# Attention in a decoder trunk: the second head's scaling behind the closing additions, and two weight casts ahead of copies at its beginning

## The chip, the cores and the metric

The kernel runs on one core of a Trainium2 chip. The metric is the device time of one execution in microseconds (us), and of several executions the median. One execution was also taken with the profiler; all rows below come from that one.

## The reference, cut to what matters

For one layer, with 2048 rows of 1024 columns, 16 query heads and 2 key/value heads of 64, and a window of 128 keys:

```python
shift, scale, gate = jnp.split(jax.nn.silu(c) @ w_ada[l] + b_ada[l], 3, axis=-1)
u = x * (1.0 + scale[:, None, :]) + shift[:, None, :]
q, k, v, a_gate, p_in, p_gate, m_a, m_p = jnp.split(u @ w_in[l], offsets, axis=-1)
a = sliding_window_sink_attention(q, k, v, sinks[l], bias, mask) * jax.nn.silu(a_gate)
a = a @ w_attn_proj[l]
p = jnp.einsum('bsgc,gcd->bsgd', multiscale_causal_pool(p_in), w_pool_mix[l]).reshape(B, S, POOL_WIDTH)
p = (p * pool_scale[l]) * jax.nn.silu(p_gate)
p = p @ w_pool_proj[l]
y = (jax.nn.sigmoid(m_a) * a + jax.nn.sigmoid(m_p) * p) @ w_out[l] * (1.0 + gate[:, None, :])
x = layer_norm(DEEPNORM_ALPHA * x + y, ln_gain[l], ln_bias[l])
```

The attention of a block of 128 queries is a softmax over 256 keys plus one sink term, with a bias by distance. The division by the softmax's sum is the scaling that this change moves.

## The kernel before, in words

All matrix products are made with 32-bit numbers that are split into a high and a low part (`low`, line 131, is the subtraction that makes the low part), and each product is three matmuls: high by high, high by low, low by high. A pair of weight rows (a "quad") is multiplied with the halves of `u` by Strassen-like sums: seven block products named B11, T1, T2, B21, T3, B22 and T4 instead of eight. Each block product is 12 matmuls of 128x512 that accumulate in a PSUM bank. After T2 comes a closing addition, b = c + p5, after T3 another, p5 = c + p5, both on VectorE. The T3 product accumulates on the same bank c that T2's addition reads, so its first matmul waits for that addition.

The sequence is computed in two halves. Each half has a stage of gate products (`ring`, with `gate_quad`, whose `consume` applies Silu to a finished product at line 585) and then an `attention` stage. In the trace the first attention stage runs from about 250 to 606 us and the second from about 826 to 1184 us.

`attention` has 67 steps of the loop over n. There are 64 units of work (8 head pairs by 8 blocks of 128 queries), and each is pipelined over four steps. In step n TensorE does, in this order: the scores of unit n (4 matmuls into bank lg), the transposes of unit n-2 (4 into bank pt, the first of the first head, the second of the second head, and so on in turn), a share of the block products of the next weights ("fill", 15 or 18 matmuls), and the value products of unit n-2 (4 into bank pv). VectorE does, in program order: the reciprocal of unit n-1's sums, the additions that gather the output of unit n-3, two passes that add the bias to unit n's scores, the low part `ptl` of unit n-2's transposed weights, and then `tensor_scalar` on `E[:, 1]`, which scales the second head of unit n-1 by that reciprocal. The first head is scaled by ScalarE. In the trace both write the tile L; the transposes of this unit in the next step read it. Behind this scaling, still in step n, the fill issues what belongs to the finished block products: closing additions, low parts of weights, and in `take_q` (for query weights) the high part of two heads on ScalarE and the low part on VectorE, 64x512 each, tile qs.

The wrapper class `Ordered` (names act, dve, pool, pe, sp) keeps an instruction where the program has it on its engine; what is issued through `nc.scalar` and the like may be moved by the scheduler.

At the beginning of `attention` (before the loop) stand the exponential on a one-element tile that loads its function table, `seed(0)` (copies the bank of B11 into the bank in which T2 accumulates), the copy `p5` of T1's bank, and `split` for the first three block products, T2, B21 and T3: a cast of the weight block to its high part on ScalarE and the low part on GpSimd.

Of the kernel before, what the change touches and what calls it, by code (L numbers as in the profile page):

```python
# [14 lines left out]
AF = mybir.ActivationFunctionType  # L15
ALU = mybir.AluOpType
# [43 lines left out]
def kernel(  # L60
# [22 lines left out]
    nc = tc.nc  # L83
    pe, act, dve, pool, sp = (Ordered(tc, e) for e in (nc.tensor, nc.scalar, nc.vector, nc.gpsimd, nc.sync))
# [45 lines left out]
    def low(engine, dst, src, hi):  # L130
        engine.tensor_tensor(dst, src, as32(hi), ALU.subtract)  # L131
# [320 lines left out]
    def defer(ticks, f):  # L452
        due.append((now[0] + ticks, len(due), f))
# [127 lines left out]
    def gate_quad(s, name, base, m, kind):  # L581
        def consume(ph, mi, t, src):
            g = ph.c("sig")
            if kind:
                nc.scalar.activation(g, src, AF.Silu)
                if kind == "scaled":
                    nc.vector.tensor_scalar(g, g, psc[:, m + mi : m + mi + 1], None, ALU.mult)
            else:
                nc.scalar.copy(g, src)
            defer(2, lambda: sp.dma_start(gates_d[name][s, m + mi, t], g))  # L590

        return Quad((win[base + m], win[base + m + 1]), consume)
# [179 lines left out]
    def attention(ph, s, fills, post, opened):  # L772
# [10 lines left out]
        def bias_tile(j):  # L783
            bt = tp.tile([P, 2, 2 * P], F32, tag="bt", bufs=2, name="bt")
            e_src = e_rep[:, 2 * j : 2 * j + 2, :]
            sp.dma_start(bt, bass.AP(e_src.tensor, e_src.offset + P - 1, [[HEADS * ET - 1, P], [ET, 2], [1, 2 * P]]))
            return bt
# [92 lines left out]
        splits = {}  # L880
# [5 lines left out]
        for x, (kind, m, _) in enumerate(fills):  # L886
            if kind == "mix" and POOL_W[m // 2] >= 8:
                on_dve |= {(x, "T3"), (x, "T4"), (x + 1, "T2"), (x + 1, "T3")}

        def split(i):  # L890
            x, name = seq[i]
            q = quads[x]
            if name == "B11" and x > 1:
                q.sum1(pool)
            w = ph.split()
            hi, lo = made[i] = w[:, 0:CH], w[:, CH:]
            act.copy(hi, q.block(name))
            low(dve if name == "T1" or (x, name) in on_dve else pool, lo, q.block(name), hi)
            if name == "T1":
                q.mid(pool)  # L900
            elif name == "B21":
                q.late(pool)
# [18 lines left out]
        def seed(x):  # L921
            st[x][2] = bank()
            act.copy(st[x][2], st[x][0])

        def ended(i):
            x, name = seq[i]
            if x >= K or name == "B11":
                return
            a, b, c, p5 = st[x]
            if name == "T1":  # L930
                p5 = st[x][3] = tp.tile([P, CH], F32, tag="p5", bufs=2, name="p5")
                act.copy(p5, b)
            elif name == "T2":
                dve.tensor_tensor(b, c, p5, ALU.add)
            elif name == "T3":
                dve.tensor_tensor(p5, c, p5, ALU.add)
            elif name == "B21":
                take(x, 0, 0, a)
            elif name == "B22":
                take(x, 0, 1, b)  # L940
            else:
                take(x, 1, 0, c)
                take(x, 1, 1, p5, True)
# [40 lines left out]
        U = 2 * NB  # L984
        load_kv(s)
        bts = {0: bias_tile(0)}
        act.activation(warm, mhalf, AF.Exp)
        seed(0)
        p5 = st[0][3] = tp.tile([P, CH], F32, tag="p5", bufs=2, name="p5")
        act.copy(p5, st[0][1])  # L990
        for i in range(-3, 0):
            for j in splits.get(i, ()):
                split(j)
        fill = filling()
        lgs, exps, Ls, pvs, outs, ags = {}, {}, {}, {}, {}, {}
        total, done = 4 * len(seq), 0
# [1 line left out]
        for n in range(N + 3):  # L998
            now_n[0] = n
            j, t, b = n // U, n // NB % 2, n % NB  # L1000
            if n < N:
                lgs[n] = score_mms(j, n % U, b, qs[j, t])
            pt = None
            if n - 2 in Ls:
                L, k0 = Ls.pop(n - 2)
                pt = turn_mms(L, k0)
            if n - 1 in exps:
                sm = exps[n - 1][2]
                dve.reciprocal(sm, sm)
            if n - 3 in pvs:  # L1010
                pv = pvs.pop(n - 3)
                jj, tt, bb = (n - 3) // U, (n - 3) // NB % 2, (n - 3) % NB
                if bb == 0:
                    outs[jj, tt] = tp.tile([P, CH], F32, tag="o", bufs=2, name="o")
                if bb == 1:
                    ags[jj, tt] = ld("ag", gates_d["ag"][s, jj, tt], 1)
                o2 = tp.tile([HD, 2, P], F32, tag="o2", bufs=1, name="o2")
                act.copy(o2, pv[HD:])
                for h in range(2):
                    dve.tensor_tensor(  # L1020
                        outs[jj, tt][h * HD : (h + 1) * HD, bb * P : (bb + 1) * P], pv[0:HD, h, :], o2[:, h, :], ALU.add
                    )
            if n - 1 in exps:
                E, e0, sm = exps[n - 1]
                act.activation(E[:, 0, e0:256], E[:, 0, e0:256], AF.Copy, scale=sm[:, 0:1])
            if pt is not None:
                h0 = k0 // P
                pth = tp.tile([P, 2, 2, P], F32R, tag="pth", bufs=1, name="pth")
                ptl = tp.tile([P, 2, 2, P], F32R, tag="ptl", bufs=1, name="ptl")
                act.copy(pth[:, h0:], pt[:, h0:])  # L1030
            if n < N:
                lg, c0 = lgs.pop(n)
                L = tp.tile([P, 2, 260], F32, tag="L", bufs=3, name="L")
                nm = tp.tile([P, 2], F32, tag="nm", bufs=4, name="nm")
                sm = tp.tile([P, 2], F32, tag="sm", bufs=4, name="sm")
                act.copy(L[:, :, 256], nsink[:, 2 * j : 2 * j + 2])
                for h in range(2):
                    dve.tensor_tensor_reduce(
                        L[:, h, c0:256],
                        lg[:, h, c0:],  # L1040
                        bts[j][:, h, c0:],
                        1.0,
                        nsink[:, 2 * j + h : 2 * j + h + 1],
                        ALU.add,
                        ALU.min,
                        nm[:, h : h + 1],
                    )
                    act.activation(
                        L[:, h, c0:257],
                        L[:, h, c0:257],  # L1050
                        AF.Exp,
                        bias=nm[:, h : h + 1],
                        scale=-1.0,
                        accum_out=sm[:, h : h + 1],
                    )
                exps[n] = (L, c0, sm)
            if pt is not None:
                low(dve, ptl[:, h0:], pt[:, h0:], pth[:, h0:])
            if n - 1 in exps:
                E, e0, sm = exps.pop(n - 1)  # L1060
                dve.tensor_scalar(E[:, 1, e0:256], E[:, 1, e0:256], sm[:, 1:2], None, ALU.mult)
                Ls[n - 1] = (E, e0)
            while done < -(-total * (n + 1) // (N + 3)):
                next(fill)
                done += 1
            if pt is not None:
                pvs[n - 2] = value_mms((n - 2) % U, k0, pth, ptl)
            run_coming()
            if n % U == 2 and j + 1 < KT:
                bts[j + 1] = bias_tile(j + 1)  # L1070
            for x in [x for x in outs if n == x[0] * U + x[1] * NB + NB + 2]:
                o = outs.pop(x)
                pool.tensor_tensor(o, o, ags.pop(x), ALU.mult)
                later(n + 1, lambda x=x, o=o: keep_raw(ain_d[s], *x, o))
            if n == 28:
                if s:
                    sp.dma_start(as32(kk[:, :, 0:P]), k_d[0, :, :, 2 * CH :])
                sp.dma_start(as32(kk[:, :, P : P + CH]), k_d[s, :, :, P : P + CH])
            if n == 30:
                if s:  # L1080
                    sp.dma_start(as32(vv[:, 0]), v_d[0, :, 2 * NB])
                sp.dma_start(as32(vv[:, 1 : 1 + NB]), v_d[s, :, 1 : 1 + NB])
            if n == 31:
                sp.dma_start(as32(kk[:, :, P + CH :]), k_d[s, :, :, P + CH :])
            if n == 33:
                sp.dma_start(as32(vv[:, 1 + NB :]), v_d[s, :, 1 + NB :])
# [465 lines left out]
    with Pools("mix", spare=4, p=2, c=8) as ph:  # L1552
# [10 lines left out]
        for n, (raw, i) in enumerate((raw, i) for raw in (ain_d[1], pin_d[1], wo_d) for i in range(4)):  # L1563
            for offset, f in sums_to(ph, raw, i, load_raw(raw, i)):
                at = int(2 + 8 * n + offset)
                i, gi = every[at // 14]
# [78 lines left out]
```

## Time and profile before

| what | value |
|---|---|
| median of 3 runs | 1693.99 us (1690.03 to 1697.75) |
| the profiled execution | 1691.31 us |
| its span, first to last instruction | 1689.5 us |
| TensorE busy | 1647.0 us, 97% |
| VectorE busy | 1204.8 us, 71% |
| ScalarE busy | 1021.7 us, 60% |
| GpSimd busy | 995.3 us, 59% |
| granted TensorE clock, mean | 0.996 |

The span and the busy times are from the profiled execution, whose own time lies 1.8 us above its span. PE is TensorE, PEld its weight loads, DVE VectorE, ACT ScalarE, POOL GpSimd. In a row of the timeline stand the start, the length, the engine, the line, the operation, the written tile, an arrow, the tiles read, and how many instructions the row joins; in brackets how long the engine had been idle before it and what it waited for. Most rows show line 56, a helper's line, so that the tiles' names tell the operation.

### The profile page before, as it was taken

What the parts mean: (1) busy time and instruction counts of PE and PEld (TensorE: products, weight loads), DVE (VectorE), ACT (ScalarE), POOL (GpSimd) and SP (SyncE); (2) the same over time, 40 slices, a digit from 0 to 9 for tenths busy, and PEclk for the clock granted to TensorE, in tenths of its full rate; (3) what the DMA queues carried; (4) which work ended last, traced back from release to release, by engine and by line L of the source; (5) the groups of instructions that cost most, each with busy time, mean ns of one, the idle gap of its engine ahead of it and who ended that gap; (6) DMA issues with size and microseconds to landing.
All of it is one profiled execution on the core that took longest, in us unless ns stands there. A gap on an engine that the chain in (4) does not pass through costs nothing.

```text
span 1689.5 us, 24673 instructions
## 1 busy us (share of the span) xinstructions
PE 1647.0 (97%) x8058; PEld 1384.2 (82%) x8058; DVE 1204.8 (71%) x2140; ACT 1021.7 (60%) x2142; POOL 995.3 (59%) x734
## 2 busy tenths in 40 slices
PE   7999999999999999999999999999999999999997
PEld 6788888888888888888788888888878877888886
DVE  6955655776857657357467677675679997989877
ACT  4644547778777756334578777776546445645452
POOL 3343347586866838762376858587567667533442
PEclk9999999999999999999999999999999999999999
DMA  9688843333423468875542334223979797878443
GB/s 360 203 260 310 212 162 107 113 126 112 150 100 107 131 233 312 271 242 181 198 138 87 126 130 136 102 93 131 325 250 392 257 372 255 323 274 280 150 150 113
DMA packets 188850, 336.80 MB, mean 199 GB/s; under 512 B 18336, under 2 KB 44080, under 8 KB 188720
## 3 DMA queue, kind: packets, MB, share of 16 engines
q1 hardware_dynamic: 185600, 330.96, 57.2%
q10 hardware_dynamic: 3088, 4.23, 1.1%
q8 instruction: 64, 1.05, 0.2%
q14 instruction: 66, 0.54, 0.1%
q0 software_dynamic: 32, 0.02, 0.0%
HBM read 227.96 MB, written 110.33 MB: 200 GB/s over the span
## 4 chain that ended last, share of the span: by engine, by line
PE 67%; DVE 12%; DMA 7%; issue 5%; ACT 5%; POOL 4%; SPq 1%; POOLq 0%; DVEq 0%; ACTq 0%
PE mm L56 44%; PE lg L56 16%; PE pv L56 4%; PE pt L56 3%; DVE w_set L131 3%; DVE set_T L56 2%; DVE set_B L56 1%; ACT L L56 1%; DMA g<-ma_d 1%; DMA g<-mp_d 1%; POOL spare L56 1%; DVE w_set L56 1%; ACT w_set L56 1%; DVE wide L627 1%; DMA W<-in_win_dram 1%
## 5 line engine op out<-in xcount | busy, mean ns | idle before, releaser
L56 PE MATMUL mm<-set_B,w_set 128*128 128x512 f32 x2664 | 655.3, 393 | 2.2 <-DVE w_set L131 1.6
L56 PEld LDWEIGHTS mm<-set_B,w_set 128*128 128x128 f32 x2664 | 497.1, 189 | 106.2 <-DVE w_set L131 3.0
L56 PE MATMUL mm<-set_T,w_set 128*128 128x512 f32 x1824 | 454.3, 395 | 6.3 <-DVE mm L56 3.9
L56 PE MATMUL lg<-set_T,w_set 128*128 128x512 f32 x1704 | 412.0, 391 | 10.1 <-DVE w_set L131 5.7
L56 PEld LDWEIGHTS mm<-set_T,w_set 128*128 128x128 f32 x1824 | 335.9, 188 | 76.5 <-DVE mm L56 6.5
L56 PEld LDWEIGHTS lg<-set_T,w_set 128*128 128x128 f32 x1704 | 319.5, 188 | 81.1 <-DVE w_set L131 6.9
L131 DVE TENSOR_TENSOR w_set<-W,w_set 128x1024 fp32r<-128x1024 f32 x138 | 203.2, 1474 | 137.6 <-ACT w_set L305 124.1
L305 ACT CAST w_set<-W 128x1024 fp32r<-128x1024 f32 x138 | 144.8, 1050 | 215.4 <-PE mm L56 134.1
L56 POOL TENSOR_TENSOR w_set<-W,w_set 128x512 fp32r<-128x512 f32 x120 | 157.3, 1319 | 116.5 <-ACT w_set L56 114.6
L268 POOL TENSOR_TENSOR W<-W,A 128x512 f32<-128x512 f32 x46 | 73.0, 1586 | 233.3 <-DMA A<-in_win_dram 66.1
L56 DVE TENSOR_TENSOR o<-pv,o 64x128 f32<-64x128 f32 x256 | 72.1, 282 | 133.8 <-ACT o L56 127.4
L56 POOL TENSOR_TENSOR spare<-spare 128x512 f32<-128x512 f32 x68 | 127.8, 1882 | 27.1 <-DMA spare<-pin_B 10.3
L56 POOL TENSOR_TENSOR W<-W 128x512 f32<-128x512 f32 x82 | 108.3, 1335 | 53.2 <-DVE sm L56 29.5
L56 ACT ACTIVATE L<-L,nm 128x257 f32<-128x257 f32 (+1 forms) x256 | 127.2, 499 | 9.4 <-DVE nm L56 3.6
L277 POOL TENSOR_TENSOR W<-W 128x512 f32<-128x512 f32 x46 | 74.7, 1625 | 94.6 <-DVE w_set L131 87.0
L56 DVE CUSTOM_DVE_ANT_0 L<-lg,bt,nsink 128x256 f32<-128x256 f32 (+1 forms) x256 | 111.7, 473 | 20.3 <-PE lg L56 11.3
L56 ACT CAST w_set<-W 128x512 fp32r<-128x512 f32 (+1 forms) x164 | 100.3, 626 | 20.2 <-POOL W L56 15.0
L272 POOL TENSOR_TENSOR W<-W 128x512 f32<-128x512 f32 x44 | 72.7, 1655 | 65.1 <-DVE w_set L131 53.7
L56 ACT COPY o<-pv 64x256 f32<-64x256 f32 x128 | 47.3, 370 | 76.3 <-PE pv L56 75.0
L56 DVE TENSOR_TENSOR ptl<-pt,pth 128x512 fp32r<-128x512 f32 (+1 forms) x128 | 85.7, 670 | 1.3 <-ACT pth L56 1.0
L273 POOL TENSOR_TENSOR W<-W 128x512 f32<-128x512 f32 x44 | 71.9, 1635 | 20.6 <-DMA W<-in_win_dram 17.0
L56 ACT ACTIVATE L<-L,sm 128x256 f32<-128x256 f32 (+1 forms) x128 | 64.3, 502 | 31.5 <-DVE sm L56 31.2
(230 smaller groups left out, 2398.7 us busy)
## 6 DMA issues: line engine op xcount, KB each, us to landing
W<-in_win_dram SPq DMA_DIRECT2D x42, 512.0 KB, 5.8
W<-in_win_dram SPq DMA_DIRECT2D x42, 256.0 KB, 3.8
A<-in_win_dram SPq DMA_DIRECT2D x42, 256.0 KB, 5.1
ag_d<-sig SPq DMA_DIRECT2D x32, 256.0 KB, 5.9
pg_d<-sig SPq DMA_DIRECT2D x32, 256.0 KB, 4.2
pg<-pg_d SPq DMA_DIRECT2D x32, 256.0 KB, 3.2
pin_B<-fin SPq DMA_DIRECT2D x32, 256.0 KB, 2.0
ag<-ag_d SPq DMA_DIRECT2D x32, 256.0 KB, 3.0
```

The source lines that it names most:

```text
L56: return lambda *args, **kw: self.tc.keep_in_program_order(op(*args, **kw))
L131: engine.tensor_tensor(dst, src, as32(hi), ALU.subtract)
L268: e.tensor_tensor(self.w[:, 1, :], self.w[:, 2, :], self.a22, ALU.add)
L272: e.tensor_tensor(x[:, 1, :], x[:, 1, :], x[:, 0, :], ALU.subtract)
L273: e.tensor_tensor(x[:, 2, :], x[:, 0, :], x[:, 2, :], ALU.subtract)
L277: e.tensor_tensor(x[:, 3, :], x[:, 3, :], x[:, 1, :], ALU.subtract)
L305: a.copy(by_two(hi), raw)
L627: nc.vector.tensor_tensor(dst, g, dst, ALU.add)
```

## The change

There are three edits.

- The Silu of a gate product goes through `act` instead of `nc.scalar`, so that it keeps its place in ScalarE's program order.
- In `attention` the second head's scaling is not issued at its place, but put into a list, `put_off`. It is issued at the first of these places in the same step: behind the closing addition of T2 or of T3, ahead of the next `split` of a weight block, or at the end of the step's fill, ahead of the value products.
- Ahead of the loop the casts of the first two block products (T2 and B21) stand ahead of `seed(0)`, of the exponential that loads the table, and of the copy `p5`; the third (T3) stays behind them.

```diff
-                nc.scalar.activation(g, src, AF.Silu)
+                act.activation(g, src, AF.Silu)
...
+        put_off = []
+
+        def scale_second():
+            while put_off:
+                put_off.pop()()
+
         def split(i):
+            scale_second()
             x, name = seq[i]
...
             elif name == "T2":
                 dve.tensor_tensor(b, c, p5, ALU.add)
+                scale_second()
             elif name == "T3":
                 dve.tensor_tensor(p5, c, p5, ALU.add)
+                scale_second()
...
+        for i in (-3, -2):
+            for j in splits.get(i, ()):
+                split(j)
+        seed(0)
         act.activation(warm, mhalf, AF.Exp)
-        seed(0)
         p5 = st[0][3] = tp.tile([P, CH], F32, tag="p5", bufs=2, name="p5")
         act.copy(p5, st[0][1])
-        for i in range(-3, 0):
-            for j in splits.get(i, ()):
-                split(j)
+        for j in splits.get(-1, ()):
+            split(j)
...
-                dve.tensor_scalar(E[:, 1, e0:256], E[:, 1, e0:256], sm[:, 1:2], None, ALU.mult)
+                put_off.append(
+                    lambda E=E, e0=e0, sm=sm: dve.tensor_scalar(
+                        E[:, 1, e0:256], E[:, 1, e0:256], sm[:, 1:2], None, ALU.mult
+                    )
+                )
                 Ls[n - 1] = (E, e0)
             while done < -(-total * (n + 1) // (N + 3)):
                 next(fill)
                 done += 1
+            scale_second()
```

The order of the instructions on TensorE, GpSimd and the DMA queues is unchanged. On ScalarE it changes only at the beginning of the two attention stages. On VectorE 54 of the 128 scalings move, 27 in each stage: 13 behind the closing addition of T3, 6 behind that of T2, one behind the closing step of a pooled sum, and 7 behind the low parts of query weights (six behind one pair, one behind two pairs).

First place: ScalarE at the beginning of the first attention stage. sig is the Silu of a gate product out of bank lg, warm the one-element exponential, `w_set<-W` a weight cast, `mm<-mm` the copy of `seed(0)`, p the copy p5. Before:

```order
L585 ACTIVATE sig<-mm 128x512
L56 ACT_TABLE_LOAD
L56 ACTIVATE warm<-mhalf 128x1
L585 ACT_TABLE_LOAD
L585 ACTIVATE sig<-lg 128x512 x2
L56 COPY mm<-mm 128x512
L56 COPY p_2252<-mm 128x512
L56 COPY w_set<-W 128x512 x3
L56 COPY L<-nsink 128x2
L56 ACT_TABLE_LOAD
L56 ACTIVATE L,sm<-L,nm 128x129 x2
```

The same place now:

```order
L56 ACTIVATE sig<-mm 128x512
L56 ACTIVATE sig<-lg 128x512
L56 COPY w_set<-W 128x512
L56 ACTIVATE sig<-lg 128x512
L56 COPY w_set<-W 128x512
L56 COPY mm<-mm 128x512
L56 ACT_TABLE_LOAD
L56 ACTIVATE warm<-mhalf 128x1
L56 COPY p_2259<-mm 128x512
L56 COPY w_set<-W 128x512
L56 COPY L<-nsink 128x2
L56 ACTIVATE L,sm<-L,nm 128x129 x2
```

Two of the three casts have moved ahead of `seed(0)` and between the two Silus, and of three table loads one is left.

Second place: VectorE in the step in which T4 of a query quad ends (row 642 and on in the stage before; the scaling is that of unit 48). Before:

```order
L56 TENSOR_TENSOR ptl<-pt,pth 128x512
L56 TENSOR_SCALAR L<-L,sm 128x128
L56 TENSOR_SCALAR qs_5417<-mm,qs_5417 64x512 x2
L56 TENSOR_SCALAR qs_5422<-p_5162,qs_5422 64x512 x2
L56 TENSOR_TENSOR w_set<-W,w_set 128x512
L56 RECIPROCAL sm<-sm 128x2
```

The same place now:

```order
L56 TENSOR_TENSOR ptl<-pt,pth 128x512
L56 TENSOR_SCALAR qs_5416<-mm,qs_5416 64x512 x2
L56 TENSOR_SCALAR qs_5421<-p_5161,qs_5421 64x512 x2
L56 TENSOR_SCALAR L<-L,sm 128x128
L56 TENSOR_TENSOR w_set<-W,w_set 128x512
L56 RECIPROCAL sm<-sm 128x2
```

The scaling of L has moved behind the four low parts of query weights.

Third place: VectorE where T2 of a pooled quad is closed (the scaling of unit 35). Before:

```order
L56 TENSOR_TENSOR ptl<-pt,pth 128x512
L56 TENSOR_SCALAR L<-L,sm 128x256
L56 TENSOR_TENSOR mm<-mm,p_4526 128x512
L56 TENSOR_SCALAR fin<-fin,mm 128x512
L56 RECIPROCAL sm<-sm 128x2
```

The same place now:

```order
L56 TENSOR_TENSOR ptl<-pt,pth 128x512
L56 TENSOR_TENSOR mm<-mm,p_4525 128x512
L56 TENSOR_SCALAR L<-L,sm 128x256
L56 TENSOR_SCALAR fin<-fin,mm 128x512
L56 RECIPROCAL sm<-sm 128x2
```

The closing addition of T2 now stands ahead of the scaling.

## The prediction

> **What bounds the kernel now.** I read the page first, for the engine that is hardly ever idle:
>
> ```profile
> span 1689.5 us, 24673 instructions
> PE 1647.0 (97%) x8058; PEld 1384.2 (82%) x8058; DVE 1204.8 (71%) x2140; ACT 1021.7 (60%) x2142; POOL 995.3 (59%) x734
> ```
>
> TensorE is busy for 97% of the span, so the change can only matter through the time in which TensorE waits. The second view is that of TensorE's waits in the two attention stages, since no edit acts on the order of work elsewhere. Columns: total us, times, longest us. First stage (250 to 606 us):
>
> ```profile
> PE mm L56 <- DVE mm L56: 2.3, 2, 1.5
> PE pv L56 <- DVE ptl L56: 0.8, 2, 0.6
> PE mm L56 <- ACT w_set L56: 0.8, 1, 0.8
> PE mm L56 <- POOL w_set L56: 0.6, 1, 0.6
> ```
>
> Second stage, its beginning (826 to 836 us) and the rest of it:
>
> ```profile
> PE mm L56 <- POOL w_set L56: 0.6, 1, 0.6
> PE mm L56 <- ACT w_set L56: 0.4, 1, 0.4
> ```
>
> ```profile
> PE mm L56 <- DVE mm L56: 1.6, 2, 1.1
> ```
>
> The reader is to see how little there is to win. What the change aims at is the waits for a closing addition (`DVE mm`, 2.3 and 1.6) and for the first casts (`ACT w_set` and `POOL w_set`, 1.4 and 1.0): 6.3 us in all, 0.37% of the span. The third view is the timeline around each of these waits and around each moved scaling. There one looks for the reverse: the transposes of the next step, which read the scaled tile L and have no row in these lists, so that nothing waits for the scaling now.
>
> **The beginning of a stage.** Here are ScalarE, GpSimd and TensorE in the first stage:
>
> ```profile
> 253.19 1.48 POOL L272 TENSOR_TENSOR W<-W 128x512 f32<-128x512 f32 x1
> 256.80 0.57 ACT L56 COPY mm<-mm 128x512 f32<-128x512 f32 x1 [1.68 <-PE mm L56]
> 259.46 0.59 ACT L56 COPY p<-mm 128x512 f32<-128x512 f32 x1 [2.10 <-PE mm L56]
> 259.94 1.66 ACT L56 CAST w_set<-W 128x512 fp32r<-128x512 f32 x3
> 260.62 0.73 PE L56 MATMUL mm<-set_T,w_set 128*128 128x512 f32 x2 [0.80 <-ACT w_set L56]
> 261.97 0.50 PE L56 MATMUL mm<-set_T,w_set 128*128 128x512 f32 x1 [0.62 <-POOL w_set L56]
> ```
>
> The three casts stand behind two copies that each wait for TensorE, so the first is done at about 260.5, and TensorE waits 0.80 for it and 0.62 more for GpSimd's low part. The block that is cast first is ready when GpSimd's subtraction ends, 253.19 + 1.48 = 254.67. In the new order the cast goes then (1.66 / 3 = 0.55 long), with one Silu between the two casts, all of it in ScalarE's idle time before 256.80; GpSimd, idle from 254.67, has over 4 us for its low part before TensorE asks at about 259.8. Both waits go: **-1.42** here and -0.98 (0.63 + 0.35, the list's 0.6 and 0.4) in the second stage, together -2.4. The two table loads that are dropped as well are ScalarE's time alone; TensorE asks for nothing of the exponentials in this step, so I cost them at nothing. The second Silu comes later by one cast and the wait for 254.67, some 0.8; only its scaling and its store to memory are behind it, and TensorE needs neither here.
>
> **The closing additions.** Of the 19 moved ahead of a scaling in a stage, TensorE waits for two. The first stage:
>
> ```profile
> 448.30 1.28 POOL L56 TENSOR_TENSOR w_set<-W,w_set 128x512 fp32r<-128x512 f32 x1
> 448.45 1.28 DVE L56 TENSOR_SCALAR L<-L,sm 128x256 f32<-128x256 f32 x1
> 449.65 0.69 DVE L56 TENSOR_TENSOR mm<-mm,p 128x512 f32<-128x512 f32 x1
> 450.39 0.96 PE L56 MATMUL mm<-set_T,w_set 128*128 128x512 f32 x3 [1.53 <-DVE mm L56]
> 528.23 0.34 DVE L56 TENSOR_SCALAR L<-L,sm 128x256 f32<-128x256 f32 x1
> 528.49 0.69 DVE L56 TENSOR_TENSOR mm<-mm,p 128x512 f32<-128x512 f32 x1
> 529.23 0.50 PE L56 MATMUL mm<-set_T,w_set 128*128 128x512 f32 x1 [0.77 <-DVE mm L56]
> ```
>
> At the first place the addition comes 449.65 - 448.45 = 1.20 earlier, so of 1.53 some 0.33 stays. At the second it comes only 0.26 earlier. But TensorE will arrive there later, by the wait of 2.1 that I work out below for the step before it, and VectorE has caught up by then; I take the whole 0.77, with 0.26 as the lower end. The second stage repeats this with 1.1 and 0.5 (the list): I take 0.95 and 0.5. Sum -3.4, with -2.7 as the smaller end.
>
> These rows also show why a scaling, 0.34 alone, takes 1.28 beside GpSimd: it ends 0.15 after the GpSimd instruction that ran when it began (448.30 + 1.28 = 449.58; 449.73). A moved scaling can meet GpSimd or miss it, and that is the unknown size below. [...]
>
> **What the moved scalings cost.** Behind a closing addition nothing: the two instructions change places, and the scaling ends when the addition ends now. In the tightest step that is 430.10 + 0.68 = 430.78, and the second head's transpose is asked for at 430.79 + 0.15:
>
> ```profile
> 430.10 0.68 DVE L56 TENSOR_TENSOR p<-mm,p 128x512 f32<-128x512 f32 x1
> 430.79 0.38 PE L56 MATMUL pt<-ident,L 128*128 128x128 f32 x2
> ```
>
> It is different where it goes behind the low parts of query weights (qs). That pair takes 1.39 and itself waits for ScalarE, while TensorE goes on through values and scores to the transposes (pt), whose second one, some 0.15 after the first, needs the scaling. First the step with two pairs, then four with one pair:
>
> ```profile
> 518.88 1.39 DVE L56 SCALAR_TENSOR_TENSOR qs<-mm,qs 64x512 fp32r<-64x512 f32 x2 [1.39 <-ACT qs L56]
> 519.75 0.38 PE L56 MATMUL pt<-ident,L 128*128 128x128 f32 x2
> 520.28 1.39 DVE L56 SCALAR_TENSOR_TENSOR qs<-p,qs 64x512 fp32r<-64x512 f32 x2
> 397.43 1.39 DVE L56 SCALAR_TENSOR_TENSOR qs<-mm,qs 64x512 fp32r<-64x512 f32 x2 [1.48 <-ACT qs L56]
> 398.07 0.49 PE L56 MATMUL pt<-ident,L 128*128 128x128 f32 x3
> 398.12 1.29 POOL L56 TENSOR_TENSOR w_set<-A,w_set 128x512 fp32r<-128x512 f32 x1 [2.32 <-ACT w_set L56]
> 320.27 1.39 DVE L56 SCALAR_TENSOR_TENSOR qs<-mm,qs 64x512 fp32r<-64x512 f32 x2
> 320.90 1.28 POOL L56 TENSOR_TENSOR w_set<-A,w_set 128x512 fp32r<-128x512 f32 x1 [0.81 <-ACT w_set L56]
> 321.42 0.38 PE L56 MATMUL pt<-ident,L 128*128 128x128 f32 x2
> 335.29 1.39 DVE L56 SCALAR_TENSOR_TENSOR qs<-mm,qs 64x512 fp32r<-64x512 f32 x2 [1.05 <-ACT qs L56]
> 336.57 1.28 POOL L56 TENSOR_TENSOR w_set<-W,w_set 128x512 fp32r<-128x512 f32 x1 [2.60 <-ACT w_set L56]
> 337.21 0.49 PE L56 MATMUL pt<-ident,L 128*128 128x128 f32 x3
> 412.62 1.39 DVE L56 SCALAR_TENSOR_TENSOR qs<-mm,qs 64x512 fp32r<-64x512 f32 x2 [0.72 <-ACT qs L56]
> 413.86 0.49 PE L56 MATMUL pt<-ident,L 128*128 128x128 f32 x3
> ```
>
> - Two pairs: they end at 520.28 + 1.39 = 521.67, the scaling at 522.0; TensorE wants it at 519.75 + 0.15. Wait **2.1**.
> - 397: the pair ends at 398.82; alone the scaling would end at 399.16 (wait 0.94), but GpSimd runs until 399.41, so 399.56: 1.34.
> - 320: 321.66, alone 322.0 (0.4), with GpSimd until 322.18, 322.33: 0.76.
> - 335: 336.68, alone 337.02 (no wait), with GpSimd until 337.85, 338.0: 0.64.
> - 412: 414.01 and 414.35, GpSimd not in the way: 0.34.
>
> The other two of the seven I take at nothing; one of them shows how near that is:
>
> ```profile
> 407.13 1.39 DVE L56 SCALAR_TENSOR_TENSOR qs<-mm,qs 64x512 fp32r<-64x512 f32 x2 [1.06 <-ACT qs L56]
> 409.06 0.49 PE L56 MATMUL pt<-ident,L 128*128 128x128 f32 x3
> ```
>
> The pair ends at 408.52, the scaling alone at 408.86, the transpose wants it at 409.21; a GpSimd instruction in the way could cost up to 1.3. The sum is 5.2 a stage; the second stage has the same steps in the same order, so **+10.4** for both, between 7.5 (never GpSimd) and 15.6 (the four near ones hit as well). I take 10.4, worked out with GpSimd where the rows show it.
>
> **The sum.** -2.4 - 3.4 + 10.4 = **+4.6** us. The profiled execution took 1691.31 (span 1689.5 and 1.8 around it), so 1695.9 against itself. It lies 2.7 below the median of the three runs, 1693.99; the mean of all four is 1693.3, and 1693.3 + 4.6 = **1697.9** is my forecast for a median.
>
> **The rivals.**
> - *The late scalings don't reach TensorE.* That needs a cover of 2.1 us between the fill's end and the transposes. For it: the lists show no wait for L now, and VectorE is busy only 71%. Against it: between the two stand only value products and scores, and the starts of the transposes used above come behind these. Then only the gains are left, -5.8: 1687.5.
> - *Slower, by a lock at the near ones.* The scaling meets a running GpSimd instruction in the four near steps too: + 5.2, and the sum is +9.8: 1703.1. It decides this way if three or more of the four are hit. For it: the scaling at 448 meets one now. Against it: GpSimd starts with a cast's end, and that moves with TensorE.
> - *The change doesn't do what it says at the additions*: they come no earlier because something else is then late (the product itself, or the copy p5). Then -3.4 falls away: +8.0, 1701.3. The rows at 448 speak against it, since VectorE ran the scaling back to back with the addition.
>
> **How the numbers follow.** Forecast 0.55, the lock at the near ones 0.20, additions without gain 0.12, scalings covered 0.13. The range that leaves out no more than 2 in 10 goes from 1689.5 (the low end of the forecast, with 7.5 for 10.4: 1695.0, and the runs' scatter, in which 1693.99 stands between 1690.03 and 1697.75) to 1705 (the lock, and scatter). 0.5% is 8.5 us, about what a measurement of this kernel tells from no change. Faster by more would need all of TensorE's idle time in both stages: 0.04. Slower by more comes from the lock for most of its 0.20, and a little from the others: 0.19. Within: 0.77.
>
> **What would show it.** In the new profile's list of TensorE's waits: new rows `PE pt` waiting for `DVE L`, together about 10 us, with the longest about 2.1 in the steps with two pairs of qs; no `ACT w_set` or `POOL w_set` rows at the beginnings; `DVE mm` down from 3.9 to under 1. If there are no `PE pt` rows, the first rival holds and my cost was wrong; if they sum to 15, the second. It would be wrong altogether if the time moved by more than 10 us either way, since TensorE's waits could not account for it.

## The result, and the profile after

| | before | after |
|---|---|---|
| median, 10 runs each (us) | 1694.2 (1690.03 to 1698.05) | 1703.78 (1698.88 to 1707.66) |
| the profiled execution | 1691.31 | 1702.92 |
| its span | 1689.5 | 1701.1 |

The ratio is 1.0053, with an interval of 1.0039 to 1.0067. The ratios here and below are formed from all runs, not from the two medians, and can differ from the quotient of the medians by 0.1%. The changed kernel is slower by 9.6 us between the medians, and by 9.0 (6.6 to 11.4) by the ratio; the forecast was +4.6 (1697.9), and its range, 1689.5 to 1705.0, holds 1703.78, near its upper end.

The page of after, its first rows and the group of the transposes (out<-in, count, busy us, mean ns, then the idle time ahead and what ended most of it):

```profile
span 1701.1 us, 24672 instructions
PE 1652.7 (97%) x8058; PEld 1389.7 (82%) x8058; DVE 1215.4 (71%) x2140; ACT 1017.8 (60%) x2138; POOL 994.0 (58%) x734
...
L56 PE MATMUL pt<-ident,L 128*128 128x128 f32 x496 | 78.2, 274 | 9.8 <-DVE L L56 9.7
```

The transposes had no wait for L before; now the last figure is 9.7 us. TensorE's waits in both attention stages (250 to 1190 us of after: total, times, longest):

```profile
PE pt L56 <- DVE L L56: 9.7, 10, 2.1
PE pv L56 <- DVE ptl L56: 1.6, 4, 0.6
PE lg L56 <- ACT w_set L56: 1.3, 1, 1.3
...
PE mm L56 <- DVE mm L56: 0.3, 1, 0.3
```

The waits for closing additions fell from 3.9 to 0.3, those for the first casts are gone, ten waits for the scaled L are there, and one row has no counterpart in the prediction: the scores (lg) wait 1.3 once.

To see where the profiled execution lost its 11.6 us, I cut it at two events that every version has: the first scores of the first attention stage, and the last value product of the second. The middle is the time from the start of the one row to the start of the other. Before has the first of them at 259.26 and the second at 1178.62; after has

```profile
262.43 0.56 PE L56 MATMUL lg<-kk,qs 128*128 128x128 f32 x4
...
1186.19 0.40 PE L56 MATMUL pv<-ptl,vv 128*128 128x256 f32 x2
```

So the start takes 3.2 us more, the middle (both attention stages) 4.4 more, and the end 4.0 more. TensorE's waits that the change acts on all lie in the middle, and there they add up: 9.7 - 3.6 - 2.4 + 1.1 = +4.8. The start and the end were the open question.

### The profile page after: what moved, and what is told of

It is laid out like the page before. It is cut to its first block, busy times and chain, and to the rows that moved or that the text cites. A ratio compares the mean times of both kernels' runs of the same rounds, so it can differ in the third digit from the quotient of the medians.

```text
span 1701.1 us, 24672 instructions
## 1 busy us (share of the span) xinstructions
PE 1652.7 (97%) x8058; PEld 1389.7 (82%) x8058; DVE 1215.4 (71%) x2140; ACT 1017.8 (60%) x2138; POOL 994.0 (58%) x734
## 4 chain that ended last, share of the span: by engine, by line
PE 75%; DVE 12%; ACT 5%; issue 3%; DMA 3%; POOL 1%; SPq 1%; POOLq 0%; DVEq 0%; ACTq 0%
PE mm L56 48%; PE lg L56 19%; PE pt L56 4%; PE pv L56 4%; DVE w_set L131 2%; DVE set_T L56 2%; ACT L L56 1%; DVE qs L56 1%; DMA g<-mp_d 1%; DVE L L56 1%; DVE wide L627 1%; ACT qs L56 1%; SPq L56 1%; DVE set_B L56 1%; DVE g L625 1%
## 5 line engine op out<-in xcount | busy, mean ns | idle before, releaser
L56 PE MATMUL lg<-set_T,w_set 128*128 128x512 f32 x1704 | 412.5, 392 | 11.6 <-DVE p L388 4.5
L56 POOL TENSOR_TENSOR W<-W 128x512 f32<-128x512 f32 x82 | 108.5, 1338 | 55.8 <-DVE sm L56 34.0
L277 POOL TENSOR_TENSOR W<-W 128x512 f32<-128x512 f32 x46 | 73.8, 1605 | 95.6 <-DVE w_set L131 85.5
L272 POOL TENSOR_TENSOR W<-W 128x512 f32<-128x512 f32 x44 | 74.7, 1700 | 63.3 <-DVE w_set L131 51.4
L56 PE MATMUL pt<-ident,L 128*128 128x128 f32 x496 | 78.2, 274 | 9.8 <-DVE L L56 9.7
```

The lines of the kernel that those rows point to most:

```text
L56: return lambda *args, **kw: self.tc.keep_in_program_order(op(*args, **kw))
L272: e.tensor_tensor(x[:, 1, :], x[:, 1, :], x[:, 0, :], ALU.subtract)
L277: e.tensor_tensor(x[:, 3, :], x[:, 3, :], x[:, 1, :], ALU.subtract)
```

## The experiments

The expectations name theories by letters. **A**: the time goes where TensorE waits for the late scalings behind query weights. **B**: some 5 us more come from outside the attention stages and go with the kernel. **C**: the scalings behind closing additions cost as well. **D**: the scores of the second stage wait for something else than the load of the keys. **E**: after a wait of some 2 us TensorE's clock is halved for a while, so the wait costs more than its length. **F**: the clock falls at that place whatever the wait.

### The scaling alone, and the beginnings alone

The first kernel is after without the edits on Silu and at the beginnings; the second is before with these edits alone.

```diff
-                act.activation(g, src, AF.Silu)
+                nc.scalar.activation(g, src, AF.Silu)
...
-        for i in (-3, -2):
-            for j in splits.get(i, ()):
-                split(j)
-        seed(0)
         act.activation(warm, mhalf, AF.Exp)
+        seed(0)
...
-        for j in splits.get(-1, ()):
-            split(j)
+        for i in range(-3, 0):
+            for j in splits.get(i, ()):
+                split(j)
```

> Only the second head's scaling is put off; the Silu and the casts at the beginning are as in the kernel before. Theory A (the change costs what TensorE waits for the late scalings in the two attention stages): the ten waits of transposes for the scaled tile are there, about 10 us; the waits for closing additions fall from 3.9 to under 1; the waits for the first casts stay at 2.4; the time is about 6.5 us above the kernel before, ratio 1.004. Theory B (about 5 us more come from somewhere outside the attention stages, brought by the new order on VectorE): ratio 1.007 or more.

Measured: 1703.62 against 1695.12, ratio 1.005 (1.0032 to 1.0069), between what A (1.004) and B (1.007 or more) expect. TensorE's waits in its attention stages:

```profile
PE pt L56 <- DVE L L56: 9.7, 10, 2.1
...
PE mm L56 <- POOL w_set L56: 1.2, 2, 0.6
PE mm L56 <- ACT w_set L56: 1.2, 2, 0.8
```

The second kernel undoes the list in after:

```diff
-                put_off.append(
-                    lambda E=E, e0=e0, sm=sm: dve.tensor_scalar(
-                        E[:, 1, e0:256], E[:, 1, e0:256], sm[:, 1:2], None, ALU.mult
-                    )
-                )
+                dve.tensor_scalar(E[:, 1, e0:256], E[:, 1, e0:256], sm[:, 1:2], None, ALU.mult)
```

> Only the Silu kept in order and the two casts ahead; the scaling is where it was. Theory A: no waits of transposes, the first stage's beginning gains 1.4, the second's 1.0 less the 1.1 that its first scores wait longer for the keys' load, which stands behind the store of the late Silu on SyncE's queue; together about -1.3 us, ratio 0.999. Theory B in its other form (the 5 us come with the edits on ScalarE): ratio 1.002 or more.

Measured: 1693.17 against 1695.12, ratio 0.9994 (0.998 to 1.0009). The waits for casts are gone, but 2.4 us have come back at the scores, where 1.1 more were expected:

```profile
PE lg L56 <- DMA kk<-k_end_d: 2.4, 1, 2.4
```

So the whole loss comes with the scaling, and by the list of waits the beginnings' gain of 2.4 is nearly spent again on a wait for the keys of the second stage.

### The scaling ahead of the query parts

After, with the scaling also issued ahead of a direct `take_q`, so that no low part of query weights stands ahead of it:

```diff
                 else:
+                    scale_second()
                     take_q(m + mi, t, src, act, dve)
```

> The whole change, but a scaling that is put off is issued ahead of the low parts of query weights as well, so that it goes behind closing additions only. Theory A: no waits of transposes for the scaled tile, waits for closing additions under 2 us, time 3 to 5 us below the kernel before, ratio 0.997 to 0.998. Theory C (the scalings behind closing additions cost as well, by other waits): ratio 1.000 or above.

Measured: 1692.97 against 1695.12, ratio 0.9978 (0.9963 to 0.9993). No wait for L is left in its list, though the 19 scalings behind additions in each stage stay moved:

```profile
PE lg L56 <- DMA kk<-k_end_d: 2.0, 1, 2.0
...
PE mm L56 <- DVE mm L56: 1.1, 3, 0.5
```

A holds and C falls: the seven scalings behind query parts are the loss, and without them the change is slightly faster than before. The additions keep 1.1 here against 0.3 in after: without the wait of 2.1 in the step ahead, 0.5 of the second addition's wait stays.

### The keys from ScalarE's queue

The same, with the loads of the second stage's last keys and values issued by ScalarE in place of SyncE; and that edit alone on after.

```diff
     def load_kv(s):
         if s:
-            sp.dma_start(as32(kk[:, :, 0:P]), k_end_d)
-            sp.dma_start(as32(vv[:, 0]), v_end_d)
+            act.dma_start(as32(kk[:, :, 0:P]), k_end_d)
+            act.dma_start(as32(vv[:, 0]), v_end_d)
```

> As the run before it in this call, and the two loads of the previous half's last keys and values are issued from ScalarE's queue, ahead of the two last Silus, instead of from SyncE's behind their stores. Theory A: the first scores of the second attention stage no longer wait 1.3 us, so 1.3 us less than the run before it. Rival D (the scores wait for something else that is late there, as the list's releaser, a cast on ScalarE, says): no difference.

Measured: 1686.26 against 1695.12, ratio 0.9952 (0.9935 to 0.9969). This version beats both kernels. ScalarE's queue issues the load at 820.63, the scores start at 829.09, and TensorE's list has no row for the keys; the additions wait 1.1 us, as in the version before. The issue of the load:

```profile
820.63 0.62 ACTq L56 DMA_DIRECT2D kk<-k_end_d  x1
```

> The whole change, and the loads of the previous half's keys and values from ScalarE's queue ahead of the last two Silus. Theory A: the first scores of the second attention stage don't wait for that load any more (1.3 to 1.8 us in the three profiles of the changed kernel), the ten waits for the scaled tile stay at 9.7; ratio about 1.0035 to 1.004. Rival D: no difference from the changed kernel, 1.005.

Measured on after: 1699.64 against 1695.08, ratio 1.0031 (1.0015 to 1.0046). The wait at the scores is gone here too, and the waits for L stay at 9.7. So D falls: the scores of the second stage wait for the load, wherever the list names ScalarE or the DMA. The first of the two versions gained more than the 1.3 that A expected: from 0.9978 to 0.9952 is 4.4 us, though the two intervals overlap. In the profile without this edit the wait is 2.0, and behind it 1.7 more are lost at half clock (shown at the end). The rest stays open. In both profiles with the edit the start was also short, 259.89 and 260.48, but so it was in the first profile of before (259.26), which doesn't have the edit. On after the gain can't be told from the scatter: 1.0031 (1.0015 to 1.0046) against 1.0053 and, in the repeat below, 1.0044.

### Both kernels again, to see the scatter of the start and the end

Unchanged copies of before and after, profiled again, twice each.

> The kernel before, unchanged, timed against itself. In the profiles so far the stretch from the first scores to the last value products is 919.4 us before and 923.8 after the change, but the start ahead of it took 259 to 264 us and the end behind it 510 to 515 us in kernels whose order there is the same. Theory A (start and end vary from execution to execution): ratio 1.000, the middle stretch again within 0.5 us of 919.4, while start or end differ by some us from the first profile. Theory B (start and end go with the kernel): start 259.3 and end 510.9 again.

> The changed kernel, unchanged. Theory A: the middle stretch within 0.5 us of 923.8; the ratio to the kernel before between 1.002 and 1.005, lower than the 1.0053 of the first comparison. Theory B: start 262.4 and end 514.9 again and ratio 1.005 or more.

> A third profile of the kernel before, for the same question: theory A, the middle stretch at 919.4 and a start anywhere between 259 and 264; theory B, the start at 259.3.

> A third profile of the changed kernel: theory A, the middle stretch at 923.8 and a start anywhere between 259 and 264, an end anywhere between 510 and 515; theory B, the start at 262.4 and the end at 514.9.

Measured: before repeated 1695.83 against 1695.59, ratio 1.0002 (0.9989 to 1.0014); after repeated 1701.65 against the same, 1.0044 (1.0029 to 1.006); the third profiled executions took 1697.57 and 1705.84. The three pieces of each profile, cut as above:

The last column is what the middle lost by stretches at half clock: the sum, over windows of one us, of what the granted clock lacked to 1.

| version | start | middle | end | lost at half clock in the middle |
|---|---|---|---|---|
| before | 259.26 | 919.36 | 510.88 | 0 |
| before, second | 262.79 | 918.84 | 514.77 | 0 |
| before, third | 263.70 | 918.53 | 513.57 | 0 |
| after | 262.43 | 923.76 | 514.91 | 0 |
| after, second | 262.42 | 926.62 | 515.76 | 3.4 |
| after, third | 263.40 | 927.53 | 513.17 | 3.4 |
| scaling alone | 263.98 | 925.79 | 511.43 | 0 |
| beginnings alone | 263.70 | 917.29 | 510.61 | 0 |
| scaling ahead of the query parts | 263.82 | 915.03 | 514.25 | 1.7 |
| the same, keys from ScalarE's queue | 259.89 | 912.20 | 510.11 | 0 |
| after, keys from ScalarE's queue | 260.48 | 922.88 | 512.84 | 1.7 |
| after, two-pair step undone (below) | 263.89 | 921.74 | 513.97 | 0 |

B falls: the start and the end of the kernel before vary by 4 us from execution to execution, and its first profile had both short. Between the means of three, after's start is 0.8 longer and its end 1.5; that can't be told from this scatter. The middle of before varies by 0.8 (918.5 to 919.4), that of after by 3.8 (923.8 to 927.5), so A's bound of 0.5 us held for neither. But the middles of the two kernels don't overlap: their means are 918.9 and 926.0, so +7.1.

What varies in the start is the speed of TensorE's matmuls. Three of the same kind near 24 us in the first profiles of before and of after:

```profile
24.05 0.95 PE L56 MATMUL mm<-set_B,w_set 128*128 128x512 f32 x3
```

```profile
24.93 1.63 PE L56 MATMUL mm<-set_B,w_set 128*128 128x512 f32 x3
```

In before three take 0.95 at 24.05 and 0.84 to 0.96 up to 41 us; in after they take 1.63 and 1.48, about half that speed, for some 10 us more, and 0.92 at 33.61. The second and third profiles of before do the same as after's: 1.63 at 25.14 and 25.08, and 0.85 only at 34.88 and 38.88. It is the lengths of the rows that show this: the granted clock is 1.00 at this time in the records of both.

### The step with two pairs undone

The middle of after varies by 3.8 us, and its profiles differ at the steps with the long wait. Here the scaling goes ahead of the query parts only in the step that takes two pairs:

```diff
             else:
+                kind, m, _ = fills[x]
+                if kind == "q" and 8 * (m - 1) + 7 <= now_n[0]:
+                    scale_second()
                 take(x, 1, 0, c)
```

> The whole change, but in the step with two pairs of query low parts (one a stage) the scaling stays ahead of them. Theory A: the two waits of 2.1 us go, the other eight (5.6 us in all) stay, some 0.5 us per stage of waiting for a closing addition comes back; the middle stretch is 923.8 - 4.2 + 1 = 920.6 us, ratio 1.000 to 1.002. Theory E (after the two waits of 2.1 us TensorE's clock is halved for some 3.3 us in part of the executions, 1.6 us each, as in the second and third profile of the changed kernel): no stretch at half clock behind a wait for the scaled tile, so up to 2 us more come off than by A, and the ratio lies 0.003 to 0.004 below that of the changed kernel. Rival F (the clock falls at these places whatever the wait): stretches at half clock near 526 or 1105 us again.

Measured: 1696.66 against 1695.08, ratio 1.0017 (1.0006 to 1.0028). The waits for L fell from 9.7 to 5.5, the longest is 1.2, and the middle (921.74) has no stretch at half clock:

```profile
PE pt L56 <- DVE L L56: 5.5, 8, 1.2
...
PE lg L56 <- DMA kk<-k_end_d: 1.6, 1, 1.6
PE mm L56 <- DVE mm L56: 1.1, 3, 0.5
```

The time doesn't part A from E, since 1.0017 lies in A's range and is also some 0.003 below after. The clock does, over all profiles: in the seven without this wait (three of before, this one, the beginnings alone and the two with the scaling ahead of the query parts) it stayed up at both places, 14 of 14, and in the five with it it fell at 4 of 10. So F falls. One profile alone would not show it, since the first of after kept its clock as well.

## Why the prediction was right or wrong, point by point

The direction, the place and the size of the main term were right; the sum came out about half as large as the change's cost, since two terms were missing.

**The beginnings: right for what they removed.** In the first stage of after the two casts stand where the prediction put them, behind GpSimd's W and ahead of the copy of `seed(0)`, and TensorE goes from the scores to the block product without a wait:

```profile
257.89 0.62 ACT L56 CAST w_set<-W 128x512 fp32r<-128x512 f32 x1 [2.83 <-POOL W L272]
...
259.91 0.57 ACT L56 COPY mm<-mm 128x512 f32<-128x512 f32 x1 [0.39 <-PE mm L56]
```

```profile
262.43 0.56 PE L56 MATMUL lg<-kk,qs 128*128 128x128 f32 x4
262.82 2.50 PE L56 MATMUL mm<-set_T,w_set 128*128 128x512 f32 x10
```

**The step that failed: "only its scaling and its store to memory are behind it, and TensorE needs neither here".** True of the Silu's data, but wrong of the queue. In the second stage the stores of the gates (pg_d) are issued by SyncE, and the load of the keys, kk, stands right behind the last of them in its queue; in both traces it is issued 0.05 to 0.06 us after that row ends. Before, SyncE's queue and the scores that need the keys:

```profile
819.32 10.35 SPq L56 DMA_DIRECT2D pg_d<-sig  x5
829.72 0.52 SPq L56 DMA_DIRECT2D kk<-k_end_d  x1
```

```profile
832.34 0.71 PE L56 MATMUL lg<-kk,qs 128*128 128x256 f32 x4 [0.19 <-DMA kk<-k_end_d]
```

The load is issued at 829.72, and 2.62 us later the scores start, with next to no wait. Now after, from ScalarE over VectorE and SyncE to TensorE:

```profile
832.25 0.62 ACT L56 CAST w_set<-W 128x512 fp32r<-128x512 f32 x1 [3.00 <-POOL W L272]
832.78 0.59 ACT L56 ACTIVATE sig<-lg 128x512 f32<-128x512 f32 x1
...
836.83 0.62 ACT L56 CAST w_set<-W 128x512 fp32r<-128x512 f32 x1
```

```profile
833.41 1.12 DVE L587 TENSOR_SCALAR sig<-sig,psc 128x512 f32<-128x512 f32 x1 [0.90 <-ACT sig L56]
```

```profile
823.23 11.64 SPq L56 DMA_DIRECT2D pg_d<-sig  x5
834.93 0.52 SPq L56 DMA_DIRECT2D kk<-k_end_d  x1
```

```profile
837.53 0.71 PE L56 MATMUL lg<-kk,qs 128*128 128x256 f32 x4 [1.28 <-ACT w_set L56]
```

The cast waits 3.00 us for GpSimd, the Silu stands behind the cast, its scaling ends at 833.41 + 1.12 = 834.53, and only then can SyncE pass the store and issue the load, 834.93. The scores come 2.60 us behind the issue, as before; TensorE has waited 1.28. The row names a cast on ScalarE as the releaser: the third cast ends at 836.83 + 0.62 = 837.45, right ahead of the scores. But the scores don't read it. In the version of after with the load on ScalarE's queue they start at 835.07, ahead of that same cast:

```profile
835.81 0.62 ACT L56 CAST w_set<-W 128x512 fp32r<-128x512 f32 x1
```

So the load's landing is what came last. The wait is 1.28 to 2.4 us in the six profiles that have the beginnings' edit and the load on SyncE's queue, and at most 0.7 in the four without that edit. Of the 2.4 that the beginnings gain, this takes back between nearly half and nearly all.

**The additions: right.** At the first place the wait fell from 1.53 to 0.33, the predicted rest, and the scaling now stands behind the addition:

```profile
453.32 0.69 DVE L56 TENSOR_TENSOR mm<-mm,p 128x512 f32<-128x512 f32 x1
453.92 0.55 DVE L56 TENSOR_SCALAR L<-L,sm 128x256 f32<-128x256 f32 x1
```

```profile
454.06 1.66 PE L56 MATMUL mm<-set_T,w_set 128*128 128x512 f32 x6 [0.33 <-DVE mm L56]
```

At the second the whole 0.77 went, because TensorE came late there by the wait in the step ahead; where that wait was undone (1.1 instead of 0.3), the lower end held. The rival in which the additions bring nothing falls.

**The late scalings: right, in place and size.** Predicted for the first stage 2.1, 1.34, 0.76, 0.64 and 0.34; measured 2.05, 1.24, 0.69, 0.57 and 0.37; both stages 10.4 and 9.7. The rival in which they don't reach TensorE falls. What the prediction calls a lock is what its rows at 448 show: the scaling ends 0.15 behind the GpSimd instruction that ran when it began (449.73 and 449.58). The four near steps weren't hit, so the rival of the lock there falls too, though its time, 1703.1, is almost the measured 1703.78: the waits it counts on, 15.6 in all, aren't there. That the range holds the result is in part luck, since its upper end was set for this rival. The step with two pairs, on VectorE and TensorE:

```profile
522.41 1.39 DVE L56 SCALAR_TENSOR_TENSOR qs<-mm,qs 64x512 fp32r<-64x512 f32 x2 [1.70 <-ACT qs L56]
523.83 1.41 DVE L56 SCALAR_TENSOR_TENSOR qs<-p,qs 64x512 fp32r<-64x512 f32 x2
525.27 0.29 DVE L56 TENSOR_SCALAR L<-L,sm 128x128 f32<-128x128 f32 x1
```

```profile
525.61 0.33 PE L56 MATMUL pt<-ident,L 128*128 128x128 f32 x1 [2.05 <-DVE L L56]
525.69 4.36 PE L56 MATMUL mm<-set_T,w_set 128*128 128x512 f32 x18
```

A step with GpSimd in the way, where a scaling that takes 0.34 alone takes 0.68, since it ends 0.15 behind GpSimd's instruction (400.97 + 1.26 = 402.23; 402.38):

```profile
400.28 1.39 DVE L56 SCALAR_TENSOR_TENSOR qs<-mm,qs 64x512 fp32r<-64x512 f32 x2 [1.75 <-ACT qs L56]
401.70 0.68 DVE L56 TENSOR_SCALAR L<-L,sm 128x256 f32<-128x256 f32 x1
```

```profile
400.97 1.26 POOL L56 TENSOR_TENSOR w_set<-A,w_set 128x512 fp32r<-128x512 f32 x1 [2.61 <-ACT w_set L56]
```

```profile
402.44 0.55 PE L56 MATMUL pt<-ident,L 128*128 128x128 f32 x3 [1.24 <-DVE L L56]
```

With GpSimd in the way the prediction had 1.34 here, and without it 0.94; the measured 1.24 lies nearer to 1.34. Of the 128 scalings in the trace of after, 78 began while a GpSimd instruction ran, and 65 of these ended 0.13 to 0.17 behind it; the other 50 took 0.28 to 0.36.

**Not in the sum: TensorE's clock behind a wait of two us.** The second profile of after has the same wait of 2.05, and then the same 18 matmuls take 5.89, against 4.36 in the first:

```profile
525.55 0.48 PE L56 MATMUL pt<-ident,L 128*128 128x128 f32 x1 [2.05 <-DVE L L56]
525.68 5.89 PE L56 MATMUL mm<-set_T,w_set 128*128 128x512 f32 x18
```

The table of stretches, one us each (busy us of PE, PEld, DVE, ACT and POOL with counts; then the granted clock, the DMA share and GB/s):

```profile
526.00:527.00 1.00, 1.00 (x4) 0.81 (x3) 0.92 (x5) 0.71 (x2) 0.00 (x0) 0.50 0.00 0
527.00:528.00 1.00, 1.00 (x4) 0.71 (x4) 1.00 (x6) 0.86 (x5) 0.00 (x0) 0.50 0.07 16
528.00:529.00 1.00, 1.00 (x4) 0.81 (x3) 0.47 (x3) 0.87 (x3) 0.00 (x0) 0.52 0.00 0
529.00:530.00 1.00, 1.00 (x6) 0.83 (x5) 0.00 (x0) 0.72 (x2) 0.20 (x1) 1.00 0.00 0
```

and one row of the first profile of after at the same place:

```profile
527.00:528.00 1.00, 1.00 (x6) 0.83 (x5) 1.00 (x5) 0.87 (x5) 0.00 (x0) 1.00 0.08 16
```

Four matmuls in a us instead of six, for some 3.4 us: about 1.7 us lost by the clock (5.89 - 4.36 = 1.53 of it in this row). It happened at 4 of the 10 two-pair waits in five profiles (three of after, the scaling alone, and the keys moved in after).

**The sum.** With the mean of the three profiles of after: 9.7 - 3.6 - 2.4, the scores' wait at 1.6 (1.28, 1.8 and 1.8) less the 0.2 of before, and 2.3 at half clock (0, 3.4 and 3.4) make +7.4; the middle grew by 7.1. By the ratios the change cost 9.0 us (6.6 to 11.4) in the first comparison and 7.5 (4.9 to 10.2) in the repeat, so the forecast of 4.6 fell 4.4 and 2.9 short. The two missing terms, 1.4 and 2.3, less the 0.7 by which the late scalings and the 0.2 by which the additions came out better, are 2.8 of it, and the rest is within the intervals. That the first profile's list (+4.8) came so near to the forecast is partly chance: the wait of 1.1 for the keys stood against these 0.7 and 0.2, and the clock didn't fall in that execution. How often the clock falls in executions without a profile isn't shown.

## What to carry to other kernels

An instruction that is put off costs nothing until the bottleneck engine asks for its result, so put it behind the short work that the bottleneck waits for, and ahead of everything that itself waits for another engine: that difference alone was 1.0053 against 0.9978 here. When an instruction comes later, follow not only its data but the queue in which its consumer stands: here a store that waited held back the load behind it in SyncE's queue (829.72 to 834.93), and with the two loads issued from another queue TensorE's wait for them was gone. When the profiles of two kernels differ, cut them at events that both have, and profile each kernel more than once before a cause is sought for a piece that the change doesn't touch.

## What the runs showed of the hardware

In the attention stages TensorE's clock fell to 0.50 behind waits of about 2 us in some executions and not in others: at 4 of 10 waits of 2.05 to 2.12 us for the scaled tile and at 2 of 5 waits of 1.6 to 2.4 us for the keys (the two were 1.8 and 2.0), and at none of the other waits, the longest of which was 1.6. That isn't a rule for the whole kernel: at the start of the first profile of before it fell to 0.50 at 43 us, in a stretch with many matmuls of one column and with no wait longer than 0.41. Here is a wait with the clock's fall behind it, from the version with the scaling ahead of the query parts, and a longer one without, from the beginnings alone:

```profile
833.98 0.71 PE L56 MATMUL lg<-kk,qs 128*128 128x256 f32 x4 [1.96 <-DMA kk<-k_end_d]
834.53 4.50 PE L56 MATMUL mm<-set_T,w_set 128*128 128x512 f32 x12
```

```profile
836.16 0.71 PE L56 MATMUL lg<-kk,qs 128*128 128x256 f32 x4 [2.38 <-DMA kk<-k_end_d]
836.72 2.91 PE L56 MATMUL mm<-set_T,w_set 128*128 128x512 f32 x12
```
